# Hybrid Conformer/Mamba-2 layer on one core: stored up products taken into the accumulating bank, down loads and head loads put in another order

## The chip, the cores and the metric

The kernel runs on one core of a Trainium2 chip. The metric is the device time of one execution in microseconds. The engines are TensorE (PE, with PEld for its weight loads), VectorE (DVE), ScalarE (ACT), GpSimd (POOL) and SyncE (SP); SP, ACT and POOL issue DMAs, each from a queue of its own that is worked off in order.

## The reference, cut to what matters

One layer on 1024 positions of 1024 channels, in fp32:

```python
h = layer_norm(x, ln_in_g, ln_in_b)
u = h @ w_in[l]
y_a = conformer_branch(...)          # depthwise conv of 31, norm, product
y_b = ssd_branch(...)                # Mamba-2, 32 heads, chunks of 128
h = layer_norm(DN_ALPHA * h + (sigmoid(gate_a) * y_a + sigmoid(gate_b) * y_b) @ w_o[l], ...)
def conv_ffn(h, w_up, dw_w, dw_b, w_down):        # w_up 1024 x 5632, w_down 2816 x 1024
    u = causal_dwconv(h @ w_up, dw_w, dw_b)       # 3 taps
    gate, val = jnp.split(u, 2, axis=-1)
    return (jax.nn.silu(gate) * val) @ w_down
h = layer_norm(DN_ALPHA * h + conv_ffn(h, ...), ln2_g, ln2_b)
```

## The kernel before, in words

**Arithmetic.** Each fp32 factor is split into a high part (ACT casts it) and a low part (DVE subtracts, L155 and L741), and `mm3` adds three PE products: high x high, high x low, low x high (L166 to L168). A product over 512 input channels, `product`, is thus 12 matmuls of 128x512.

**Stages**, one after the other in the trace: the head (`ln_in(0)`, the norm of x, and `first_columns`), two token mixers with their combinations (to about 1307 us), the sums of h for up (`ffn_blocks`), up, down, and the last norm.

**Up.** The product with `w_up` goes by a 2x2 block scheme with seven products instead of eight. For each of the 22 steps j, `up_rest` works on 128 gate and 128 value columns; `up_weights` loads the rows `ra` and `rb`, forms the weight sums s3, s24 and s10 on DVE and splits them. The products are named by their block of h: b11 and b21 (weights ue), t2 (w_s24), t3 (w_s3), t1 and t4 (w_s10), b22 (w_s24). They share PSUM banks: `acc` banks for b11, t2, t1 and b22 of one step, `sm` banks for t3 and t4. Between two products of one bank a partial result is copied or added out, into `s`, `uv` (value) or `ug` (gate). A step has 84 matmuls. For the first eight steps (LEAD) b11 and b21 are made in `up_first`, while h's other blocks are still being formed, and are stored to DRAM (`first_scr`); those eight steps then take 60 matmuls in `up_rest` and read the two stored halves back. In them t2 has an `sm` bank of its own, and DVE adds the stored half (L871, L877, L885). From step 8 on, one bank carries all and ACT copies (L860, L865, L875, L883). After the products, both halves of u go through a convolution of three taps (L891 on ACT, two L895 on DVE into a buffer `o`, tag "o"), silu (L905) and the gating (L906); of each pair of steps DVE forms sums for down, and POOL's queue stores them as `b11_scr`, `b2_scr`, `t32_scr`, `t41_scr`. The u tiles are a ring of three.

**Down.** Seven products p of eleven steps k each (`down`, `load`). The data of a step come back from the scratch tensors, with a slice of `w_down`, into a raw tile `dr`; `c3` and `c4` keep weight slices for later products. `c3` takes the space of the block of h that b11 and b21 used, `rows` that of t3 and t4, `c4` that of b22, so their first loads wait for the last such matmul. `rows` holds h for the residual, loaded on POOL's queue. The weights are split into `w_dn{p}_{k}`.

**Order.** The program is written in blocks and a scheduler of the framework sets the order of instructions on every engine by its own estimates and by `high_priority` offsets; each engine then works through its list strictly in that order. Tiles come from pools: `tag` and `bufs` say how many buffers rotate, and a new tile waits until the last user of its buffer is done. The pools: `wst` (tag "st", 3 buffers, raw weights), `wsp` (split weights), `up` (o, raw, s, s3), `firsts` (stored products). Space of a closed pool is given to the next, with the same kind of wait.

Of the kernel before, what the change touches and what calls it, by code (L numbers as in the profile page):

```python
# [16 lines left out]
P = 128  # L17
D = 1024
# [38 lines left out]
def kernel(  # L57
# [23 lines left out]
    wsp = ctx.enter_context(tc.tile_pool(name="wsp", bufs=3))  # L81
# [67 lines left out]
    def weights(src, name, pl=None, eng=None, bufs=None):  # L149
        with tc.high_priority(offset=4000):  # L150
            st = wst.tile([P, D], F32, tag="st", name=f"st_{name}")
            SY.dma_start(st, src)
            w = (pl or wsp).tile([P, 2, D], F32R, tag="w", bufs=bufs, name=f"w_{name}")
# [80 lines left out]
    def ln_in(hh):  # L234
        hT = big_tile(f"hT{hh}")
        with pool(f"lnin{hh}", side="right") as pl:
            first = hh == 0
            xts, gb = [], []
            with tc.high_priority(offset=6000):
                for t in range(4):  # L240
# [8 lines left out]
            if first:  # L249
                SY.dma_start(pc[:, :PC_N], pcol)  # L250
# [486 lines left out]
    def split_pair(pl, src, name, n=D, bufs=None, tag="w"):  # L737

        w = pl.tile([P, 2, n], F32R, tag=tag, bufs=bufs, name=f"w_{name}")
# [75 lines left out]
    def up_first(fp, bl, j):  # L815


        w = weights(wup[2 * j], f"ue{j}")
        ps = bank(1)
        for q, block in enumerate(("b11", "b21")):  # L820
            product(ps, lambda i: w[:, i, q * HALF : (q + 1) * HALF], bl[block], q == 0)
            f = fp.tile([P, HALF], F32, tag="first", bufs=4, name=f"first{q}_{j}")
            A.copy(f, ps)
            A.dma_start(first_scr[j][q], f)

    def up_weights(upp, j):


        with tc.high_priority(offset=2000):
            r1 = wst.tile([P, D], F32, tag="st", name=f"ra{j}")  # L830
            SY.dma_start(r1, wup[2 * j])
            if j:
                r2 = upp.tile([P, D], F32, tag="raw", bufs=3, name=f"rb{j}")
# [4 lines left out]
            ue = None if j < LEAD else split_pair(wsp, r1, f"ue{j}")  # L838
# [5 lines left out]
            w24 = split_pair(wsp, r1, f"s24_{j}")  # L844
            w10 = split_pair(wsp, r2, f"s10_{j}")
# [3 lines left out]
    def up_rest(upp, us, bl, j, before):  # L849
# [3 lines left out]
        ue, w24, w10, w3 = up_weights(upp, j)  # L853
# [3 lines left out]
        ps, pz = bank(1 if ue else 0), bank(0)  # L857
        if ue:
# [5 lines left out]
            product(ps, lambda i: w24[:, i, :HALF], bl["t2"], False)  # L864
            A.copy(s, ps)  # L865
        else:
            SY.dma_start(s, first_scr[j][0])
            SY.dma_start(ug[:, early], first_scr[j][1])
            pu = bank(0)
            product(pu, lambda i: w24[:, i, :HALF], bl["t2"], True)  # L870
            V.tensor_tensor(out=s, in0=s, in1=pu, op=ALU.add)  # L871
        product(pz, lambda i: w3[:, i], bl["t3"], True)
        product(ps, lambda i: w10[:, i, :HALF], bl["t1"], not ue)
        if ue:
            A.copy(uv[:, late], ps)  # L875
# [356 lines left out]
```

## Time and profile before

| | |
|---|---|
| median of 3 runs | 2033.85 us (2031.81 to 2035.5) |
| profiled execution | 2035.35 us, span 2033.6 us |
| PE busy | 1978.0 us, 97% of the span |
| DVE busy | 1710.7 us, 84% |
| ACT busy | 1001.8 us, 49% |
| POOL busy | 171.9 us, 8% |
| DMA | 273.51 MB, mean 134 GB/s |
| granted PE clock, mean | 0.991 |

Times in rows count from the start of the span. In a timeline row stand the start, the busy time, the engine, the line of the kernel, the operation, the tile written and the tiles read, the number of instructions, and in brackets the idle time before it with what ended it. A row of a table of windows gives the stretch, its length, each engine's busy time with its instructions, the granted PE clock (1.00 is full speed), the DMA engines' busy share and their rate. A row of waits gives engine and bank, who ended the wait, the total in us, how often, the longest. In rows of the profile the numbers in tile names are left out: `w_s` is any of w_s3, w_s10 and w_s24.

### The profile page before, as it was taken

How to read it: one execution, taken by the hardware profiler on the slowest of the kernel's cores; microseconds unless marked ns; L12 is line 12 of the kernel's file. 1: busy time of each engine (PE TensorE's matmuls, PEld its weight loads, DVE VectorE, ACT ScalarE, POOL GpSimd, SP SyncE). 2: the span in 40 equal slices, each digit the busy share in tenths (PEclk: the TensorE clock that was granted, in tenths of full speed). 3: DMA queues.
4: the chain of work that ended last, by engine and by line, in shares of the span. 5: the costliest groups of instructions: out<-in, count | busy, mean ns of one | idle time of the engine just before them, and what ended most of it. 6: DMA issues, size and time to landing. Idle time of an engine off the chain costs nothing.

```text
span 2033.6 us, 24571 instructions
## 1 busy us (share of the span) xinstructions
PE 1978.0 (97%) x9164; PEld 1628.0 (80%) x9164; DVE 1710.7 (84%) x2285; ACT 1001.8 (49%) x1448; POOL 171.9 (8%) x141
## 2 busy tenths in 40 slices
PE   6999999999999999999999999998899999989998
PEld 6888887888788888888888888887778888777886
DVE  7599999989766869999998976596998788777868
ACT  4465654556453356665454645364334445443432
POOL 2010101001400000100100130010000000010000
PEclk9999999999999999999999999999999999999999
DMA  6212233332546522222423354565342232377563
GB/s 219 93 63 94 79 102 106 99 104 101 174 133 216 195 88 77 88 85 75 127 86 107 109 166 138 188 234 202 130 153 106 99 109 99 109 258 264 175 224 109
DMA packets 97303, 273.51 MB, mean 134 GB/s; under 512 B 11168, under 2 KB 11168, under 8 KB 97184
## 3 DMA queue, kind: packets, MB, share of 16 engines
q1 hardware_dynamic: 87696, 242.06, 35.9%
q0 software_dynamic: 7184, 25.69, 3.3%
q10 hardware_dynamic: 2304, 4.20, 0.6%
q8 instruction: 72, 1.18, 0.2%
q14 instruction: 47, 0.39, 0.1%
HBM read 222.36 MB, written 49.55 MB: 134 GB/s over the span
## 4 chain that ended last, share of the span: by engine, by line
PE 66%; DVE 24%; DMA 4%; issue 4%; ACT 1%; SPq 0%; DVEq 0%; ACTq 0%
PE acc L166 17%; PE acc L168 17%; PE acc L167 17%; DVE c L420 8%; PE sm L166 3%; PE sm L167 3%; PE sm L168 3%; DVE xbc L375 2%; DMA dr<-b_scr 1%; PE acc L357 1%; PE sm L534 1%; DVE fo L895 1%; DMA st_wo<-wo 1%; PE sm L515 1%; DVE w_so L155 1%
## 5 line engine op out<-in xcount | busy, mean ns | idle before, releaser
L420 DVE SCALAR_TENSOR_TENSOR c<-v,pc,c 128x512 f32<-128x512 f32 x480 | 375.3, 805 | 7.6 <-ACT c L409 6.1
L478 POOL TENSOR_TENSOR au<-seg_mv,head_of 128x1024 fp32r<-128x1024 f32 x32 | 76.3, 2383 | 962.2 <-PE sm L487 730.4
L166 PE MATMUL acc<-hT,w_c 128*128 128x512 f32 x352 | 141.1, 401 | 0.0
L167 PE MATMUL acc<-hT,w_c 128*128 128x512 f32 x352 | 140.7, 400 | 0.0
L168 PE MATMUL acc<-hT,w_c 128*128 128x512 f32 x352 | 138.5, 393 | 0.0
L895 DVE SCALAR_TENSOR_TENSOR fo<-u,pc,fo 128x1024 f32<-128x1024 f32 x88 | 111.5, 1279 | 8.5 <-ACT fo L891 7.8
L375 DVE SCALAR_TENSOR_TENSOR xbc<-u,pc,xbc 128x512 f32<-128x512 f32 x144 | 109.7, 774 | 0.7 <-ACT xbc L373 0.5
L167 PE MATMUL acc<-w_z,hT 128*128 128x512 f32 x256 | 100.9, 394 | 0.0
L166 PE MATMUL acc<-w_z,hT 128*128 128x512 f32 x256 | 100.9, 401 | 0.0
L168 PE MATMUL acc<-w_z,hT 128*128 128x512 f32 x256 | 100.7, 396 | 0.0
L1021 ACT CAST w_dn<-dr 128x1024 fp32r<-128x1024 f32 (+1 forms) x73 | 60.8, 842 | 77.7 <-DVE dr L951 31.5
L154 ACT CAST w_c<-st_c 128x1024 fp32r<-128x1024 f32 x50 | 52.5, 1051 | 86.8 <-PE acc L168 66.1
L1022 DVE TENSOR_TENSOR w_dn<-dr,w_dn 128x1024 fp32r<-128x1024 f32 (+1 forms) x73 | 69.6, 963 | 17.6 <-ACT w_dn L1021 17.5
L167 PEld LDWEIGHTS acc<-hT,w_c 128*128 128x128 f32 x352 | 66.2, 188 | 16.8 <-issue 3.8
L168 PEld LDWEIGHTS acc<-hT,w_c 128*128 128x128 f32 x352 | 66.1, 188 | 16.0 <-issue 2.6
L166 PEld LDWEIGHTS acc<-hT,w_c 128*128 128x128 f32 x352 | 66.1, 188 | 15.9 <-issue 2.6
L155 DVE TENSOR_TENSOR w_c<-st_c,w_c 128x1024 fp32r<-128x1024 f32 x47 | 60.6, 1289 | 20.2 <-ACT w_c L154 20.2
L166 PE MATMUL acc<-h1s,w_s 128*128 128x512 f32 x168 | 66.6, 397 | 5.7 <-ACT u L875 5.7
L166 PE MATMUL acc<-h1b,w_ue 128*128 128x512 f32 x176 | 68.9, 392 | 2.6 <-ACT w_ue L740 1.4
L166 PE MATMUL sm<-h1b,w_s 128*128 128x512 f32 x176 | 70.3, 400 | 0.0
L167 PE MATMUL sm<-h1b,w_s 128*128 128x512 f32 x176 | 70.3, 399 | 0.0
L168 PE MATMUL sm<-h1b,w_s 128*128 128x512 f32 x176 | 69.9, 397 | 0.0
(352 smaller groups left out, 5811.1 us busy)
## 6 DMA issues: line engine op xcount, KB each, us to landing
st_c<-wcol SPq DMA_DIRECT2D x50, 512.0 KB, 3.5
st_z<-wz SPq DMA_DIRECT2D x32, 512.0 KB, 3.4
st_wo<-wo SPq DMA_DIRECT2D x24, 512.0 KB, 3.8
ra<-wup SPq DMA_DIRECT2D x22, 512.0 KB, 3.6
rb<-wup SPq DMA_DIRECT2D x22, 512.0 KB, 3.4
t_scr<-fo POOLq DMA_DIRECT2D x22, 512.0 KB, 4.2
dr<-t_scr SPq DMA_DIRECT2D x44, 256.0 KB, 3.4
dr<-wdown SPq DMA_DIRECT2D x38, 256.0 KB, 3.8
```

The source lines that it names most:

```text
L154: A.copy(w[:, 0, :], st)
L155: (eng or V).tensor_tensor(out=w[:, 1, :], in0=st, in1=w[:, 0, :].bitcast(F32), op=ALU.subtract)
L166: TE.matmul(ps, wa(0), xa(0), start=start, stop=False, skip_group_check=more)
L167: TE.matmul(ps, wa(0), xa(1), start=False, stop=False, skip_group_check=more)
L168: TE.matmul(ps, wa(1), xa(0), start=False, stop=stop, skip_group_check=more)
L357: TE.matmul(ps[:, ts], w[:, i, k * P : (k + 1) * P], hT[:, j, k, ts], start=n == 0 and k == 0, stop=n == 2 and k == KD - 1,)
L375: V.scalar_tensor_tensor(out=o, in0=u[:, k : k + HALF], scalar=pc[:, wc + k : wc + k + 1], in1=o, op0=ALU.mult, op1=ALU.add,)
L420: V.scalar_tensor_tensor(out=accs[i], in0=v[:, k : k + HALF], scalar=pc[:, wc + k : wc + k + 1], in1=accs[i], op0=ALU.mult, op1=ALU.add,)
L478: G.tensor_tensor(out=au, in0=seg_mv[:, c, :].unsqueeze(1).to_broadcast([P, 8, P]), in1=head_of[:, g, :].unsqueeze(2).to_broadcast([P, 8, P]),
L895: V.scalar_tensor_tensor(out=o, in0=u[:, k : k + T], scalar=pc[:, wc + k : wc + k + 1], in1=o, op0=ALU.mult, op1=ALU.add,)
L1021: A.copy(w[:, 0, cs], src)
L1022: V.tensor_tensor(out=w[:, 1, cs], in0=src, in1=w[:, 0, cs].bitcast(F32), op=ALU.subtract)
```

## The change

Lines of the changed kernel carry other numbers (mm3 is L173 to L175 there, `split_pair` L754 and L755).

1. **Stored steps.** One DMA brings both stored halves into `ug`; ACT copies the late half into the accumulating bank (L892), t2, t1 and b22 all add into that bank, and ACT copies out between them, as in the later steps. DVE's three additions go.
2. **First weights.** The pool `up` is opened before `up_first`, `up_weights` of step 0 is called before the stored products of step 6, and those of steps 6 and 7 take their weights from `o` buffers. The stored products have 2 buffers instead of 4.
3. **Slots.** The parts in `wsp` get three fixed slots in turn instead of a ring of three; `raw` has 2 buffers instead of 3, `o` 4 instead of 3.
4. **Down.** Raw tiles come from nine buffers (st 3, raw 2, o 4) instead of six; five `c3` slices are copied by GpSimd from `w_st` instead of loaded a second time; the rows come in 16 half tiles at k = 4 of p = 0, 1, 2, 4; the last norm's rows are loaded by POOL's queue at p = 2.
5. **Head.** The norm rows are loaded second and third, ahead of x1; 60 transposes of the identity are put on PE at the start; the first three low weight parts are made by DVE instead of GpSimd.

```diff
+        n_parts[0] += 1
+        return wsp.tile([P, 2, D], F32R, tag=f"w{n_parts[0] % 3}", name=f"w_{name}")
...
-                    if first and t == 1:
+                    if first and t == 0:
                         gb = [row(pl, RW_ING, D, "in_g"), row(pl, RW_INB, D, "in_b")]
...
+                    for i in range(60):
+                        TE.transpose(pt[:, i % 4 * P : (i % 4 + 1) * P], ident, ident)
...
-        ws = [weights(wcol[ct], f"c{hh}_{ct}", eng=None if hh else G) for ct in cts]
+        ws = [weights(wcol[ct], f"c{hh}_{ct}", eng=None) for ct in cts]
...
-            f = fp.tile([P, HALF], F32, tag="first", bufs=4, name=f"first{q}_{j}")
+            f = fp.tile([P, HALF], F32, tag="first", bufs=2, name=f"first{q}_{j}")
...
-        ps, pz = bank(1 if ue else 0), bank(0)
+        ps, pz = bank(1), bank(0)
...
-            product(ps, lambda i: w24[:, i, :HALF], bl["t2"], False)
-            A.copy(s, ps)
         else:
-            SY.dma_start(s, first_scr[j][0])
-            SY.dma_start(ug[:, early], first_scr[j][1])
-            pu = bank(0)
-            product(pu, lambda i: w24[:, i, :HALF], bl["t2"], True)
-            V.tensor_tensor(out=s, in0=s, in1=pu, op=ALU.add)
+            with tc.high_priority(offset=2500):
+                SY.dma_start(
+                    ug[:, 2 : 2 + T].rearrange("p (q n) -> p q n", q=2),
+                    first_scr[j].rearrange("q p n -> p q n"),
+                )
+            A.copy(ps, ug[:, late])
+        product(ps, lambda i: w24[:, i, :HALF], bl["t2"], False)
+        A.copy(s, ps)
         product(pz, lambda i: w3[:, i], bl["t3"], True)
-        product(ps, lambda i: w10[:, i, :HALF], bl["t1"], not ue)
-        if ue:
-            A.copy(uv[:, late], ps)
-        else:
-            V.tensor_tensor(out=uv[:, late], in0=s, in1=ps, op=ALU.add)
+        product(ps, lambda i: w10[:, i, :HALF], bl["t1"], False)
+        A.copy(uv[:, late], ps)
...
         product(ps, lambda i: w24[:, i, HALF:], bl["b22"], False)
-        if ue:
-            A.copy(ug[:, late], ps)
-        else:
-            V.tensor_tensor(out=ug[:, late], in0=s, in1=ps, op=ALU.add)
+        A.copy(ug[:, late], ps)
...
-            o = upp.tile([P, T], F32, tag="o", bufs=3, name=f"fo{jj}")
+            o = upp.tile([P, T], F32, tag="o", bufs=4, name=f"fo{jj}")
...
+            t0, cs = {0: (0, E), 1: (0, L), 2: (4, L), 4: (4, E)}[p]
+            for t in range(t0, t0 + 4):
+                G.dma_start(rs[t][:, cs], h1_scr[t * P : (t + 1) * P, cs])
...
-            pl, tag = ((wst, "st"), (upp, "raw"))[n_raw % 2]
+            pl, tag, n = ((wst, "st", 3), (upp, "raw", 2), (wst, "st", 3), (upp, "o", 4))[n_raw % 4]
...
                 if p == 0 and k < EARLY:
                     SY.dma_start(w_st, a11)
-                    G.dma_start(c3[k], a11)
+                    G.tensor_copy(c3[k], w_st)
...
-                if k == 2 and p in (0, 2):
-                    load_rows(range(2 * p, 2 * p + 4))
+                if k == 4 and p in (0, 1, 2, 4):
+                    load_rows(p)
...
     with pool("firsts", side="right") as fp:
         for j in range(LEAD):
-            up_first(fp, bl, j)
+            if j == LEAD - 2:
+                ws = up_weights(upp, 0)
+            up_first(upp, fp, bl, j)
```

What this does to the order on three engines. First PE in the fourth stored step (j = 3), at t1 (weights w_s10_3, block h1s2). Before, it starts a bank of its own behind step 2's t4:

```order
L167 MATMUL sm516_11432<-h1b2_10852,w_s10_2_11424 128x512
L168 MATMUL sm516_11432<-h1b2_10852,w_s10_2_11424 128x512
L166 MATMUL sm518_11531<-h1s2_10449,w_s10_3_11524 128x512 [waits DVE_49,Activation_49]
L167 MATMUL sm518_11531<-h1s2_10449,w_s10_3_11524 128x512
L168 MATMUL sm518_11531<-h1s2_10449,w_s10_3_11524 128x512 [waits DVE_49]
```

Now it stands right behind t2 in the same bank (acc516):

```order
L174 MATMUL acc516_11591<-h1s3_10511,w_s24_3_11581 128x512
L175 MATMUL acc516_11591<-h1s3_10511,w_s24_3_11581 128x512
L173 MATMUL acc516_11591<-h1s2_10510,w_s10_3_11584 128x512 [waits Activation_49]
L174 MATMUL acc516_11591<-h1s2_10510,w_s10_3_11584 128x512
L175 MATMUL acc516_11591<-h1s2_10510,w_s10_3_11584 128x512 [waits DVE_49]
```

ACT's copy of s now lies between two neighbours on PE. Second, SP's queue at the start of down (dr_k is the raw tile of the k-th down step, counted from 1; each is filled by a load of data and, for the first five, one of weights). Before:

```order
L979 DMA dr_4_13948<-b11_scr3_137 128x512
L981 DMA dr_4_13948<-wdown 128x512
L979 DMA dr_3_13925<-b11_scr2_136 128x512
L981 DMA dr_3_13925<-wdown 128x512
L985 DMA c3_13866<-wdown 128x512 x6
L979 DMA dr_6_13986<-b11_scr5_139 128x512
L979 DMA dr_5_13967<-b11_scr4_138 128x512
L981 DMA dr_5_13967<-wdown 128x512
L979 DMA dr_7_14006<-b11_scr6_140 128x512
L988 DMA c4_0_13868<-wdown 128x512
```

Now, from c4_0 on (ahead of it stand dr_2, dr_4, five c3 loads, dr_1, dr_5, dr_6 and dr_9):

```order
L1013 DMA c4_0_13919<-wdown 128x512
L1013 DMA c4_1_13920<-wdown 128x512
L1013 DMA c4_2_13921<-wdown 128x512
L1013 DMA c4_3_13922<-wdown 128x512
L1013 DMA c4_4_13923<-wdown 128x512
L1013 DMA c4_5_13924<-wdown 128x512
L1004 DMA dr_8_14077<-b11_scr7_141 128x512
L1013 DMA c4_6_13925<-wdown 128x512
L1004 DMA dr_10_14117<-b11_scr9_143 128x512
L1013 DMA c4_7_13926<-wdown 128x512
L1004 DMA dr_3_13976<-b11_scr2_136 128x512
L1006 DMA dr_3_13976<-wdown 128x512
```

dr_3, whose tile is an `o` buffer now, has moved from ahead of the c3 loads to behind eight of the c4 loads. Third, ACT at the same place, with the cast of w_dn0_2 from dr_3. Before:

```order
L1021 CAST w_dn0_7_14029<-c3_13866 128x512 [waits DMAHW0_49]
L883 COPY u0_11200<-acc572_13739 128x512
L1021 CAST w_dn0_2_13929<-dr_3_13925 128x1024 [waits DMAHW5_49,PE_49]
L891 ACTIVATE fo21_13833<-u0_11200,pc_107 128x1024 [waits DMASW4_49,Activation_49]
L891 ACTIVATE fo43_13837<-u1_11201,pc_107 128x1024 [waits DVE_49]
L1021 CAST w_dn0_4_13971<-dr_5_13967 128x1024 [waits DMAHW6_49,DMAHW5_49,PE_49]
```

Now:

```order
L902 COPY u0_10969<-acc565_13794 128x512
L908 ACTIVATE fo21_13888<-u0_10969,pc_107 128x1024 [waits DMASW6_49,Activation_49]
L908 ACTIVATE fo43_13892<-u1_10970,pc_107 128x1024 [waits DMASW7_49,DVE_49]
L1045 CAST w_dn0_4_14018<-dr_5_14014 128x1024 [waits DMAHW3_49,DMAHW2_49,PE_49]
L1045 CAST w_dn0_6_14060<-c3_13917 128x512 [waits PE_49]
L1045 CAST w_dn0_7_14080<-dr_8_14077 128x512 [waits DMAHW4_49]
L922 ACTIVATE fo21_13888<-fo21_13888,pc_107 128x1024 [waits DVE_49]
L1045 CAST w_dn0_2_13980<-dr_3_13976 128x1024 [waits DMAHW1_49,DMAHW0_49]
```

The cast has moved behind the last step's convolution outputs and silu. On PE, w_dn0_2's matmuls follow those of w_dn0_0 and w_dn0_1 in both kernels.

More of the change, by code (lines that the diff above doesn't have):

```diff
@@ L249, in ln_in @@
             if first:
+                with tc.high_priority(offset=8000):
+                    pt = bank(1)
+                    for i in range(60):
+                        TE.transpose(pt[:, i % 4 * P : (i % 4 + 1) * P], ident, ident)
                 SY.dma_start(pc[:, :PC_N], pcol)
@@ L832, in up_weights @@
             if j:
-                r2 = upp.tile([P, D], F32, tag="raw", bufs=3, name=f"rb{j}")
+                r2 = upp.tile([P, D], F32, tag="raw", bufs=2, name=f"rb{j}")
             else:
@@ L1013, in load @@
                     own = n_steps % 2 and n_steps > 2
[L1014 to L1016 removed]
+                    nm = f"w_dn{p}_{k}"
+                    w = dp.tile([P, 2, D], F32R, tag="w", bufs=3, name=nm) if own else part_tile(nm[2:])
                 cuts = ((slice(0, D), st),) if w_st is not c3[k] and w_st is not c4[k] else (
@@ L1118 @@
         bl = ffn_blocks(tp, qp, mixT)
-    with pool("firsts", side="right") as fp:
-        for j in range(LEAD):
-            up_first(fp, bl, j)
     upp = ctx.enter_context(pool("up"))
@@ L1125 @@
         G.memset(u[:, :2], 0.0)
+    with pool("firsts", side="right") as fp:
+        for j in range(LEAD):
+            if j == LEAD - 2:
+                ws = up_weights(upp, 0)
+            up_first(upp, fp, bl, j)
     before = None
     for j in range(NF):
-        before = up_rest(upp, us, bl, j, before)
+        before, ws = up_rest(upp, us, bl, j, before, ws), None
     ffn_stack.close()
     dp = ctx.enter_context(pool("down", side="right"))
-    g, b = row(dp, RW_2G, D, "ln2_g"), row(dp, RW_2B, D, "ln2_b")
-    down(upp, dp, g, b)
+    down(upp, dp)
 _OUT = "out_0_dram"
```

61 lines of the change are left out of this document (38 added, 23 removed).

## Prediction

> **What bounds the kernel now.** I read the page first (PE is busy for 97% of the span, so only stretches in which PE loses matmuls are worth anything), then a table of windows of 25 us, then PE's waits, and last the timelines around the places found. All rows are of the profiled execution of the kernel before, 2035.35 us with a span of 2033.6; the median of the runs is 2033.85, 1.5 us lower, and a difference found here is applied to that median. A run can tell a change from none at 0.2%, about 4.1 us.
>
> ```profile
> core 0: us, PE busy (x) PEld busy (x) DVE busy (x) ACT busy (x) POOL busy (x), PEclk, DMA share, GB/s
> 1375.00:1400.00 25.00, 23.84 (x110) 19.48 (x109) 15.34 (x21) 13.09 (x23) 2.73 (x5) 1.00 0.63 225
> 1400.00:1425.00 25.00, 19.70 (x75) 15.61 (x74) 17.51 (x25) 6.09 (x8) 0.00 (x0) 0.86 0.46 158
> 1425.00:1450.00 25.00, 23.16 (x99) 18.09 (x98) 22.49 (x26) 12.89 (x12) 0.73 (x1) 1.00 0.34 113
> 1450.00:1475.00 25.00, 21.12 (x84) 16.86 (x83) 23.34 (x30) 6.69 (x7) 2.15 (x4) 0.90 0.42 155
> 1475.00:1500.00 25.00, 24.27 (x103) 19.53 (x102) 23.50 (x29) 10.08 (x10) 1.59 (x3) 0.97 0.49 165
> 1500.00:1525.00 25.00, 23.36 (x103) 18.90 (x102) 24.39 (x30) 10.08 (x11) 1.44 (x3) 1.00 0.42 138
> ...
> 1775.00:1800.00 25.00, 23.88 (x106) 19.40 (x104) 17.61 (x21) 10.49 (x13) 4.31 (x8) 1.00 0.59 200
> 1800.00:1825.00 25.00, 20.68 (x83) 16.69 (x84) 21.89 (x24) 14.59 (x20) 4.80 (x9) 0.86 0.72 261
> 1825.00:1850.00 25.00, 22.50 (x91) 17.83 (x90) 16.28 (x26) 9.44 (x17) 1.60 (x3) 0.93 0.88 329
> 1850.00:1875.00 25.00, 25.00 (x112) 20.69 (x111) 22.26 (x34) 9.74 (x14) 0.00 (x0) 1.00 0.78 240
> ```
>
> A full window holds 112 matmuls of 128x512 (the last row), so one costs 25/112 = 0.223 us. From 1375 to 1525, the start of up and the steps fed from stored products, PE issues 574 of 672: 98 are missing, 21.9 us. From 1775 to 1850, where up ends and down begins, 280 of 336: 56 missing, 12.5 us. These two stretches are all that the up and down parts of the change can win; the waits name what opens the holes.
>
> ```profile
> PE sm L166 <- DVE u L877: 7.0, 3, 3.9
> PE sm L166 <- ACT w_s L740: 6.0, 2, 5.3
> PE acc L166 <- ACT u L875: 5.7, 2, 5.4
> ```
>
> **Part 1, the start of up and the eight stored steps.** The first hole is the cast of the first `w_s3`; its tiles lie in space that the last stored products still held.
>
> ```profile
> 1405.84 0.79 PE L166 MATMUL sm<-h1s,w_s 128*128 128x512 f32 x1 [5.30 <-ACT w_s L740]
> 1402.21 0.69 DVE L741 TENSOR_TENSOR w_s<-s,w_s 128x512 fp32r<-128x512 f32 x1 [9.94 <-ACT w_s L740]
> L877 DVE TENSOR_TENSOR u<-s,sm 128x512 f32<-128x512 f32 x7 | 4.8, 684 | 0.6 <-PE sm L168 0.6
> ra<-wup SPq DMA_DIRECT2D x22, 512.0 KB, 3.6
> ```
>
> DVE stood idle for 9.94 us here. With the pool opened earlier that time serves the first weights, and the hole of 5.3 us with its slow matmuls goes. What is late next is the low part of `ue1_6`: it now follows s3 and the sum in `rb0` on DVE, and st_ue7's load waits for a slot of `st`; I allow 2 us (bounds 0 and the old 5.3).
>
> In each of the eight steps DVE loses L871, L877 and L885: 24 x 0.684 = 16.4 us of an engine that is 22.5 to 24.4 us busy in a window of 25. These are off the path except where PE waits for L877. ACT gains four copies of about 0.59 us a step (row of L875 below, 128x512), 19 us over eight steps on an engine that is at most 13.1 us busy in those windows. But each copy now stands between two products of one bank, and PE's order puts t1 the next product right behind the one that is copied out at three places of the stored steps (j = 1, 3, 5) and two matmuls behind it at four (j = 3 to 6). The trace has that case once, at the end of step 19.
>
> ```profile
> 1769.10 0.39 PE L167 MATMUL acc<-h1s,w_s 128*128 128x512 f32 x1
> 1769.76 0.50 PE L166 MATMUL acc<-h1s,w_s 128*128 128x512 f32 x1 [0.28 <-ACT u L875]
> 1769.12 0.59 ACT L875 COPY u<-acc 128x512 f32<-128x512 f32 x1 [1.68 <-PE acc L168]
> ```
>
> Starts 0.66 us apart instead of 0.223: 0.44 us for two matmuls between, so 0.44 + 2 x 0.223 = 0.88 with none. Three times 0.88 and, in the stored steps, four times 0.44 make 4.4 us.
>
> The remaining term is a chain that comes round every two steps. I add it up with the durations of such rows as the ones shown here and below: on DVE 1.2 for 1024 columns (two passes in 2.48) and 0.6 for 512 in a row of them, on ACT 1.15, 1.05 and 0.6. From the low part of an even step's w_s10: this and two passes (3.6), on ACT the silu, the next convolution output, the cast of w_s3 and the copy of s (3.5), on PE t1, ten matmuls of s3 and b22 (34 x 0.223 = 7.6), and on ACT the cast of the next w_s10 into the slot that b22 has left (1.1): 15.8. From there, in the odd step: six operations of 1024 and two of 512 columns on DVE up to the second pass over uv of step j-2 (8.4), the load of both halves, which SP can issue only then (512 KB, as ra: 3.6), the copy into PSUM (0.6) and the cast behind it on ACT (1.05): 13.6. Together 29.4, or 14.7 a step, against 13.4 for 60 matmuls and 0.6 of the gaps above: 0.7 x 6 = 4.2 us more (bounds: 0, if the loads come early; 10, if DVE stays the bound as now). Sum: 2 + 4.4 + 4.2 = 10.6, say 11 of the 21.9 us stay; **-11** (-16 to -5). Three slots for the parts and two for raw only shift loads: covered by this slack of about 2 us.
>
> For j of 8 and more the code is as before, but four more places have two matmuls between (10, 13, 16, 20, with 19 as before): 4 x 0.44, **+2** (0 to +3).
>
> **Part 2, from up to down.** The second hole is an ACT that stands at a convolution output because its `o` buffer waits for stores of step 19.
>
> ```profile
> 1798.77 1.15 ACT L891 ACTIVATE fo<-u,pc 128x1024 f32<-128x1024 f32 x1 [4.06 <-DMA b_scr<-fo]
> 1801.51 1.15 ACT L891 ACTIVATE fo<-u,pc 128x1024 f32<-128x1024 f32 x1 [1.59 <-DMA t_scr<-fo]
> 1804.27 0.79 PE L166 MATMUL acc<-h1s,w_s 128*128 128x512 f32 x1 [5.39 <-ACT u L875]
> 1804.86 0.63 PE L167 MATMUL acc<-h1s,w_s 128*128 128x512 f32 x1
> ...
> 1807.42 0.53 PE L167 MATMUL acc<-h1s,w_s 128*128 128x512 f32 x1
> ```
>
> After such a hole eight matmuls come 0.43 us apart (six from 1804.86 to 1807.42), 1.7 us more. With four `o` buffers this wait goes: step 20's first output needs no store, only its second waits for a store of step 19, and between c3's space coming free, which those stores follow on POOL, and ACT's wait PE has 64 matmuls, 14 us; I count the store as landed by then. But look at what SP does. `dr_3`, the data of the third down step, is given an `o` buffer, and its load now stands behind the c4 loads, which wait for the space of the last b22 product (call its end T; 1808.9 here). Before, it was loaded 34 us ahead of T, and its cast ran without a wait at 1812.86.
>
> ```profile
> SPq L988 <- PE acc L168: 14.0, 1, 14.0
> 1775.16 0.33 SPq L979 DMA_DIRECT2D dr<-b_scr  x1
> 1808.91 2.70 SPq L988 DMA_DIRECT2D c<-wdown  x6
> 1812.86 1.05 ACT L1021 CAST w_dn<-dr 128x1024 fp32r<-128x1024 f32 x1
> 1819.93 0.63 ACT L1021 CAST w_dn<-dr 128x512 fp32r<-128x512 f32 x1 [1.96 <-DMA dr<-b_scr]
> 1823.85 0.62 ACT L1021 CAST w_dn<-dr 128x512 fp32r<-128x512 f32 x1 [2.25 <-DMA dr<-b_scr]
> 1831.65 0.62 ACT L1021 CAST w_dn<-dr 128x512 fp32r<-128x512 f32 x1 [4.76 <-DMA dr<-b_scr]
> ```
>
> PE reaches `w_dn0_2` 27 matmuls after T (12 of t4, 15 of the first two down steps): T + 6.0. The last three rows are the 7th, 9th and 13th transfer of SP after T, of 256 KB each: 11.0, 14.9 and 22.7 us after T, 1.95 us apiece. `dr_3`'s two halves become the 11th and 12th: T + 20.8 at that pace, since the rows move at the same time on POOL's queue (1809 to 1832):
>
> ```profile
> q1 hardware_dynamic: 2033, 4.01, 51.3%
> q0 software_dynamic: 1124, 4.08, 44.6%
> rows<-h_scr POOLq DMA_DIRECT2D x8, 512.0 KB, 12.4
> ```
>
> The rows become half tiles, so they will crowd SP less, and 2.25 MB (five c3 copies, two norm rows) no longer go by DMA near here. Alone, the 3.1 MB through `dr_3` at the rate of these 23 us (8.1 MB, 352 GB/s) would land near T + 10. I take T + 17, nearer to the measured pace. Cast 1.05 and handover 0.1: PE waits 12.1 us, and 1.7 us of slow matmuls follow. To this come 1.8 (at j = 21 t2, t1 and b22 follow each other without a matmul between: 2 x 0.88) and 0.7 (`dr_1` now behind five c3 loads): 16.3 against 12.5, **+4** (-3 with T + 10, +8 with T + 20.8). The c3 copies on GpSimd cost at most what its sums of that shape take:
>
> ```profile
> L627 POOL TENSOR_TENSOR mean<-mean,cc 128x512 f32<-128x512 f32 x12 | 19.0, 1587 | 2.9 <-DMA cc<-c_scr 2.1
> ```
>
> Three stand ahead of step 19's stores on POOL, 4.8 us, under some 23 us of up that PE still has then; if they took 3 us longer, ACT would wait for the store again. The norm rows of the last layer norm are used 150 us later.
>
> The Trainium skill, "DMA: Bandwidth & Descriptors", section on queues, rings and completion order, says that an engine takes turns between queues packet by packet. The trace agrees: 4.01 MB in 2033 packets on SP's queue against 4.08 MB in 1124 on POOL's, with SP getting the smaller share while both were full. By it halved rows raise SP's share from 0.35 (packets of 1.97 KB against 3.63) to 0.5, 1.37 us apiece, and with two landed before the rows start `dr_3` would be there at T + 16.7, and the sum 0.3 us lower.
>
> **Part 3, the head.**
>
> ```profile
> 8.83 2.48 DVE L227 SCALAR_TENSOR_TENSOR x<-x,mv_in,in_g 128x1024 f32<-128x1024 f32 x2 [1.58 <-DMA in_g<-prow]
> 17.99 5.12 DVE L227 SCALAR_TENSOR_TENSOR x<-x,mv_in,in_g 128x1024 f32<-128x1024 f32 x2
> 16.31 9.06 POOL L155 TENSOR_TENSOR w_c<-st_c,w_c 128x1024 fp32r<-128x1024 f32 x3 [13.87 <-ACT w_c L154]
> ```
>
> The norm rows a place earlier save at most the wait of 1.58. Three low parts move to DVE, 3 x 1.2 = 3.6 us, and POOL no longer doubles DVE's passes beside it (5.12 against 2.48, and some of L230): even. Sixty transposes end before x0's are due at about 10 us or delay them by a few us, while DVE's passes over x2 and x3 set the end. **-0.5** (-2 to +1).
>
> **Sum**: -11 + 2 + 4 - 0.5 = -5.5: 2029.85 for the profiled execution, 2028.4 for the median.
>
> **Rivals.**
> - A, much faster. `dr_3` is there when PE comes, since c4's space comes free by an earlier product than b22's in the new layout of the pools, so that T lies some 10 us earlier for SP: the 13.8 us of Part 2 go, 2014.6. Against it speaks that L988 waited for b22 and that c4 keeps its place in the program; for it, that the two norm rows that lay ahead of c4 in that space are gone.
> - B, no change. The pace of 1.95 us holds (T + 20.8, +3.8): 2032.2. The same comes out if the chain of Part 1 eats its gain (+4 to +5). For it: both queues were full for 20 us.
> - C, slower. ACT's queue becomes the bound of the stored steps: the copy into PSUM waits for a load, and everything behind it on ACT (w_s10's cast, u's copies, the convolution) stands too. Each us over 14.7 a step costs 7; from 1.4 us over it the whole is slower by more than 4.1, at 2 us it is 2042. For it: ACT already waited for DVE and DMA in the rows above; against it: DVE gets 16.4 us of room.
>
> **How the numbers follow.** Forecast 0.40 (faster by 4 to 11), A 0.14, B 0.24, C 0.16, and 0.06 for a slower outcome by something unseen (loads in down with other slots). Faster 0.54, same 0.24, slower 0.22. The forecast's own range is 2023 to 2030; the range for 8 in 10 takes in A's 2014.6 and most of C: 2014 to 2040.
>
> **What would show it.** In the profile after: no wait of PE for w_s at the first s3 and no slow matmuls after it, some 620 matmuls between 1375 and 1525; small waits of PE for ACT s and u, 0.4 to 0.9 us each; no ACT wait of 4 us for b_scr before the end of up; and a hole in PE of 8 to 15 us at the third down step, released by ACT's cast of `w_dn`, itself waiting for dr<-b_scr. If that hole is missing, A holds; if PE's waits for ACT in the stored steps add to over 12 us, C. Wrong altogether would be a new hole in a place where nothing was lost before, in the mixers or after 1850.

## The result: 12 us slower

The changed kernel takes 2046.6 us (median of 4, 2044.9 to 2050.6), the kernel before 2034.7 beside it: a ratio of 1.0062, 95% interval 1.0042 to 1.0082. The forecast was 2028.4, and its range ended at 2040. The profiled execution after takes 2044.85 us with a span of 2043.2.

The windows of 25 us after, with the columns as before:

```profile
core 0: us, PE busy (x) PEld busy (x) DVE busy (x) ACT busy (x) POOL busy (x), PEclk, DMA share, GB/s
1375.00:1400.00 25.00, 22.09 (x91) 16.36 (x90) 20.44 (x29) 15.68 (x25) 1.80 (x5) 1.00 0.80 262
...
1425.00:1450.00 25.00, 21.61 (x86) 17.23 (x87) 22.70 (x27) 13.26 (x16) 1.23 (x2) 0.93 0.40 133
...
1800.00:1825.00 25.00, 10.94 (x47) 8.36 (x45) 14.41 (x16) 9.95 (x13) 9.27 (x17) 0.83 0.76 265
1825.00:1850.00 25.00, 21.90 (x88) 17.71 (x89) 13.39 (x20) 8.99 (x16) 2.23 (x4) 0.90 0.74 263
1850.00:1875.00 25.00, 25.00 (x112) 20.67 (x112) 19.95 (x33) 10.58 (x17) 0.55 (x1) 1.00 0.60 198
```

The window behind the end of up holds 47 matmuls of 112 (83 before); the one from 1425 holds 86 (99 before). PE's waits after, the largest of up and down:

```profile
PE acc L173 <- ACT w_dn L1045: 17.5, 2, 15.2
PE sm L173 <- ACT w_s L754: 4.4, 5, 1.6
PE acc L173 <- ACT u L897: 4.0, 2, 3.3
PE acc L173 <- ACT s L894: 3.5, 7, 0.8
PE acc L173 <- ACT w_s L754: 3.4, 4, 1.0
```

VectorE's `u`, which led the list before, is gone; ScalarE leads it, and the cast of one down weight alone costs 15.2 us. The rows of SP, ACT and PE around it:

```profile
1805.58 2.71 SPq L1013 DMA_DIRECT2D c<-wdown  x6
...
1812.18 0.33 SPq L1004 DMA_DIRECT2D dr<-b_scr  x1
1812.86 0.33 SPq L1006 DMA_DIRECT2D dr<-wdown  x1
...
1825.77 1.04 ACT L1045 CAST w_dn<-dr 128x1024 fp32r<-128x1024 f32 x1 [8.36 <-DMA dr<-wdown]
...
1811.28 0.39 PE L175 MATMUL acc<-w_dn 128*128 128x512 f32 x1
1826.87 1.65 PE L173 MATMUL acc<-w_dn 128*128 128x512 f32 x3 [15.20 <-ACT w_dn L1045]
```

The c4 loads start at 1805.58 (T); `dr_3` is issued behind eight of them and its cast starts at T + 20.2.

To compare kernels whose stages shift, I count PE's matmuls from the first product of `w_ue` on (2788 to the end in every kernel) and add up by how much starts lie further apart than 0.2236 us (distances over 0.28). Up to matmul 240 is the start of up, to 660 the stored steps, to 1740 steps 8 to 20, to 1872 the end of up (its last product), to 2300 the first part of down; behind 2300 nothing is lost anywhere. Ratios are to the kernel before in the same comparison, whose medians lie between 2032.9 and 2034.7.

| kernel | median us | ratio (95%) | 0-240 | 240-660 | 660-1740 | 1740-1872 | 1872-2300 |
|---|---|---|---|---|---|---|---|
| before | 2034.7 | | 10.2 | 12.6 | 2.3 | 7.3 | 5.0 |
| after | 2046.6 | 1.0062 (1.0042-1.0082) | 5.6 | 13.9 | 8.0 | 4.6 | 18.6 |
| e1, no o for down | 2045.2 | 1.0069 (1.0056-1.0083) | 5.4 | 13.8 | 7.9 | 4.5 | 18.0 |
| e2, ring | 2043.9 | 1.0058 (1.0046-1.0071) | 3.6 | 15.2 | 10.1 | 0.5 | 19.3 |
| e3, both | 2045.9 | 1.0066 (1.0054-1.0079) | 4.3 | 16.1 | 10.1 | 0.5 | 20.1 |
| e4, head only | 2031.6 | 0.9990 (0.9981-0.9999) | 10.0 | 12.4 | 2.2 | 7.1 | 5.4 |
| e5, before, two raw | 2036.5 | 1.0018 (1.0008-1.0029) | 0.5 | 13.8 | 1.7 | 6.9 | 17.0 |
| e6, three raw, ring | 2051.9 | 1.0087 (1.0070-1.0105) | 24.3 | 16.0 | 10.4 | 0.5 | 2.3 |
| e7, stored steps only | 2038.4 | 1.0020 (1.0010-1.0030) | 4.9 | 12.6 | 10.4 | 5.8 | 4.9 |
| e8, after without them | 2032.9 | 1.0003 (0.9993-1.0014) | 5.7 | 7.4 | 2.5 | 4.0 | 17.7 |
| e9, e8 and half slots | 2017.0 | 0.9919 (0.9906-0.9932) | 5.8 | 7.9 | 2.7 | 3.3 | 1.3 |
| e10, four stored steps | 2032.3 | 0.9993 (0.9982-1.0003) | 4.9 | 15.4 | 2.2 | 8.9 | 3.6 |
| e11, before, half slots | 2027.6 | 0.9969 (0.9958-0.9979) | 0.6 | 15.4 | 1.7 | 7.0 | 8.2 |
| e12, e11 with four o | 2020.1 | 0.9937 (0.9925-0.9949) | 10.7 | 8.3 | 5.3 | 0.5 | 3.2 |
| e13, e9, copy into bank | 2021.8 | 0.9939 (0.9925-0.9953) | 6.6 | 11.9 | 4.0 | 3.2 | 1.7 |
| e14, after, half slots | 2027.3 | 0.9966 (0.9953-0.9978) | 5.3 | 13.8 | 9.5 | 2.3 | 1.5 |

After against before: -4.6, +1.3, +5.7, -2.7 and +13.6, together +13.3. Ahead of the first `w_ue` product profiles scatter (it starts between 1348.6 and 1353.3 us, in kernels with the head edit and without), so the stages are compared and not the spans. A profiled run need not be the median one either: that of e7 took 2034.46 us, that of e12 2023.04.

### The profile page after: what moved, and what is told of

It is laid out like the page before. It is cut to its first block, busy times and chain, and to the rows that moved or that the text cites. A ratio compares the mean times of both kernels' runs of the same rounds, so it can differ in the third digit from the quotient of the medians.

```text
span 2043.2 us, 24653 instructions
## 1 busy us (share of the span) xinstructions
PE 1985.5 (97%) x9224; PEld 1629.8 (80%) x9224; DVE 1698.6 (83%) x2264; ACT 1019.8 (50%) x1480; POOL 171.9 (8%) x148
## 4 chain that ended last, share of the span: by engine, by line
PE 66%; DVE 23%; issue 4%; DMA 3%; ACT 3%; SPq 0%; POOL 0%; ACTq 0%; DVEq 0%; POOLq 0%
PE acc L173 17%; PE acc L175 17%; PE acc L174 17%; DVE c L431 8%; PE sm L173 3%; PE sm L175 3%; PE sm L174 3%; PE acc L368 2%; DVE xbc L386 2%; PE sm L545 1%; DVE fo L912 1%; DMA dr<-wdown 1%; DMA st_wo<-wo 1%; PE sm L199 1%; PE sm L526 1%
## 5 line engine op out<-in xcount | busy, mean ns | idle before, releaser
L173 PE MATMUL acc<-hT,w_c 128*128 128x512 f32 x352 | 141.0, 401 | 0.0
L175 PE MATMUL acc<-hT,w_c 128*128 128x512 f32 x352 | 138.4, 393 | 0.0
L173 PE MATMUL acc<-h1s,w_s 128*128 128x512 f32 x264 | 105.5, 400 | 11.6 <-ACT u L897 4.0
L175 PE MATMUL acc<-h1s,w_s 128*128 128x512 f32 x264 | 104.1, 394 | 1.6 <-DVE w_s L755 1.6
L174 PE MATMUL acc<-h1s,w_s 128*128 128x512 f32 x264 | 103.6, 392 | 0.0
L173 PE MATMUL acc<-w_z,hT 128*128 128x512 f32 x256 | 100.8, 401 | 0.0
L175 PE MATMUL acc<-w_z,hT 128*128 128x512 f32 x256 | 100.7, 396 | 0.0
L162 DVE TENSOR_TENSOR w_c<-st_c,w_c 128x1024 fp32r<-128x1024 f32 x50 | 64.0, 1282 | 20.2 <-ACT w_c L161 20.2
L173 PE MATMUL acc<-w_dn 128*128 128x512 f32 x160 | 62.2, 397 | 17.5 <-ACT w_dn L1045 17.5
L175 PEld LDWEIGHTS acc<-hT,w_c 128*128 128x128 f32 x352 | 66.1, 188 | 16.1 <-issue 2.6
L173 PEld LDWEIGHTS acc<-hT,w_c 128*128 128x128 f32 x352 | 66.1, 188 | 16.0 <-issue 2.6
L173 PE MATMUL sm<-h1b,w_s 128*128 128x512 f32 x176 | 69.7, 396 | 4.4 <-ACT w_s L754 4.4
```

Of the source, the lines that this page charges most:

```text
L162: (eng or V).tensor_tensor(out=w[:, 1, :], in0=st, in1=w[:, 0, :].bitcast(F32), op=ALU.subtract)
L173: TE.matmul(ps, wa(0), xa(0), start=start, stop=False, skip_group_check=more)
L174: TE.matmul(ps, wa(0), xa(1), start=False, stop=False, skip_group_check=more)
L175: TE.matmul(ps, wa(1), xa(0), start=False, stop=stop, skip_group_check=more)
```

## Experiments

**First theory: two accidents, the o slot of `dr_3` and the fixed slots of the parts (e1, e2, e3), and the head by itself (e4).** A line of a diff can stand for several places; `...` marks what is left out of it.

```diff
- ((wst, "st", 3), (upp, "raw", 2), (wst, "st", 3), (upp, "o", 4))[n_raw % 4]
+ ((wst, "st", 3), (upp, "raw", 2))[n_raw % 2]                        # e1, e3
- wsp.tile([P, 2, D], F32R, tag=f"w{n_parts[0] % 3}", ...)
+ wsp.tile([P, 2, D], F32R, tag="w", bufs=3, ...)                     # e2, e3
```

> The changed kernel, but the loads of the down steps take turns between st and raw alone; none goes into an o buffer, so dr_3 is again issued ahead of the c4 loads. Theory (the 15.59 us hole of PE at the third down step, with the half clock behind it, comes from dr_3 standing behind c4 in SP's queue): the hole goes, of PE's 17.5 us of waits for the casts of w_dn at most 4 stay, and the time is 13 to 17 us below the changed kernel: 2030 to 2034. Rival (the loads around the end of up are late because SP's and POOL's queues are both full, wherever dr_3 stands): a hole of 8 us or more stays at one of the first four down steps, and the time is above 2038.

> The changed kernel, but the weight parts take the next free slot of a ring of three again, in place of three fixed slots in turn. Theory (steps 8 to 21 lost 7.4 us against before because a fixed slot ties the cast of a weight part to the one part that held this slot, and sets products of one bank two matmuls apart): the waits of PE for ACT's s, u and w_s in steps 8 to 21 fall to what they were before, 5 to 8 us are won, 2038.5 to 2041.5; the hole at the third down step stays at 14 to 17 us. Rival (the loss of these steps comes from the four o buffers and two raw buffers): no change, 2045 to 2048.

> Both edits: the ring for the weight parts, and no o buffer for the down loads. If the two losses are separate places and add, 19 to 23 us below the changed kernel: 2024 to 2028, which is 7 to 11 us below the kernel before. If one only moves the other (weights that come earlier meet the same late loads), 2030 to 2034.

> The kernel before with the head's part of the change alone: norm rows loaded second, sixty transposes of the identity at the start, low parts of the first weights on VectorE. Theory (the head is worth what the start of the first 128x512 product showed, -0.28 us): 2033.5 to 2034.5, no change that can be measured. Rival (the 2.6 us that the changed kernel was ahead at 660 us come with this part as well, through another order of VectorE's passes there): 2030.5 to 2032.

Both theories fell. In e1 `dr_3` is ahead of c4 and its hole is gone, but the loss in down stays (18.0 against 18.6):

```profile
PE acc L173 <- ACT w_dn L1045: 10.3, 4, 7.1
PE acc L174 <- DVE w_dn L1046: 3.0, 2, 2.1
...
1827.68 0.62 ACT L1045 CAST w_dn<-dr 128x512 fp32r<-128x512 f32 x1 [7.83 <-DMA dr<-b_scr]
```

The hole moved from the third to the seventh down step (`dr_7`), and a second one opened some 87 us after T. So the loads are one too few, whichever of them stands behind c4. The ring of e2 makes steps 8 to 20 no better (10.1), and e3, with both edits, lies outside both of its ranges. The head is worth 1.4 us, within what a run can tell; the median of e4 lies in the range of its rival, and PE's wait for VectorE's `x` at 662 us (1.13 us in the kernel before) is indeed gone in e4.

**What raw has to do with it (e5, e6).** e5 is the kernel before with one thing taken away; e6 is the changed kernel with three raw, for which the copies of the first products move into the slots of `s`, with the ring of e2 and the down loads in st and raw in turn.

```diff
- tag="raw", bufs=3          # up_weights of before; raw() of the down loads likewise
+ tag="raw", bufs=2          # e5
- f = fp.tile([P, HALF], F32, tag="first", bufs=2, ...)
+ f = upp.tile([P, HALF], F32, tag="s", bufs=2, ...)    # e6, with raw bufs=3
```

> The kernel before with two raw buffers instead of three, in up and for the down loads, and nothing else. Theory (the changed kernel loses because one raw buffer went: one down load fewer is ahead of the c4 loads, six b11_scr rows where there were seven, and a 2D step of two loads waits for the slot again later): PE loses 4 to 8 us more within 40 us of the end of up, as the variant without o for the down loads did, and 3 to 8 us some 85 us after it; together 7 to 14 us slower than before, 2040 to 2047. Rival (the lost buffer is covered; what costs is the order of the casts or the row loads): within 2 us of before.

> The changed kernel with three raw buffers beside the four o buffers: the copies of the first products take the slots of s, so that the pool firsts goes and its space holds the third raw. The weight parts stand in a ring of three, and the down loads take st and raw in turn. Theory (the third raw buffer is what the changed kernel lacks): the holes at the third down step, 14 us after the end of up and 85 us after it go (PE's waits for the casts of w_dn under 5 us), while ScalarE's wait for b_scr stays away: against the kernel before 3 to 4 us won in the stored steps, 6 to 7 at the end of up, 0 to 8 lost in steps 8 to 21: 2023 to 2032. Rival (the losses at the down steps come from elsewhere): 2038 or more.

In down both came out as the theory said: two raw cost the kernel before 12.0 us there (17.0 against 5.0), three raw bring the changed kernel to 2.3 (e3, with the ring and the down loads as in e6 but two raw, loses 20.1). Of e5, the casts that PE waits for:

```profile
PE acc L166 <- ACT w_dn L1021: 5.5, 4, 1.8
PE sm L166 <- ACT w_dn L1021: 4.8, 1, 4.8
```

The totals came out otherwise. e5 is only 3.5 us slower than before, because the hole at the first `w_s3` closed by itself (0.5 against 10.2): without the third raw the pool of up is 4 KB smaller, and these tiles, as I read it, no longer lie on the space of the last stored products. No run prints where tiles lie, but e11 and e12 below bear it out: their one difference is a fourth o buffer of the same 4 KB, and the hole is closed in the first (0.6) and open in the second (10.7). e6 loses 24 us at the start of up; in its order the first copies of stored products stand on ScalarE behind the last casts of the blocks (one such wait of PE is 10.8 us). That was my edit's fault, and says nothing on the change.

**The stored steps by themselves (e7) and the change without them (e8).** In e7 `up_rest` alone is the changed one; in e8 all is changed but it: two loads, t2 and t1 in banks of their own, VectorE's three sums.

> The kernel before with the stored steps of the changed one: one load of both halves, the stored product copied into the accumulating bank by ScalarE, no passes of VectorE over s. Prediction on record: these copies free VectorE of 16.4 us, and the waits for its u go. If so, 5 to 10 us less than before in the stored steps: 2023 to 2028. Rival from the cumulative losses (between the 240th and the 660th matmul of up the changed kernel loses 13.8 us, before 12.7): the edit wins nothing by itself, since waits for ScalarE's s and u and for the casts behind them take the place of those for VectorE: 2031 to 2035.

> The changed kernel, but with the stored steps of the kernel before (two loads, products into a bank of their own, sums by VectorE); the early first weights, the slots and the down part stay as changed. If the stored-step edit wins nothing, the losses up to the 660th matmul of up stay at 17 to 22 us and the time at 2043 to 2049, unless the other order of the loads moves the hole at the third down step. If it is what won 11 us, 2055 or more.

e8 is the run that turned the study. Without the stored-step edit the stored steps lose 7.4 us in place of 13.9, and steps 8 to 20, which the edit does not touch, 2.5 in place of 8.0; the whole is 13.7 us faster than the changed kernel by the medians, 12 by the ratios; both ranges of the expectation had it slower. In e7 the loss in the first hole falls from 10.2 to 4.9, that in steps 8 to 20 rises from 2.3 to 10.4, and that in the stored steps stays at 12.6; its median lies above both of its ranges.

The lead of e8 over before in the stored steps (7.4 against 12.6) goes with another part of the change, as the table shows: with the old stored steps, kernels of three o buffers lose 12.4 to 15.4 us there (before, e4, e5, e11), those of four 7.4 to 8.3 (e8, e9, e12), and e12 differs from e11 by the fourth o alone and has the first weights as before. How that buffer does it was not tried.

**What carries the loss into steps 8 to 20 (e10).** The order of PE's instructions is fixed before the run. In steps 8 and on the code is the same in all kernels but for the buffers, but the order is a pattern that repeats, and the stored steps set which one. The pattern around the start of `ue.14` (matmuls in brackets; t4.12 is step 12's fourth product):

```
before, e10: b22.12(11) t4.12(12) b22.12(1) t2.13(12) ue.14(24)
e7, e2:      t2.13(10) b22.12(11) t4.12(12) b22.12(1) t2.13(2) ue.14(4)
```

In e7 `ue` follows three matmuls behind t4. ScalarE casts w_s10 only when t4 has ended, and the cast of `w_ue` stands behind that one; ACT and PE of e7, and its waits from 1525 to 1785 us:

```profile
1599.23 1.05 ACT L740 CAST w_s<-rb 128x1024 fp32r<-128x1024 f32 x1 [9.71 <-PE sm L168]
1600.18 1.04 ACT L740 CAST w_ue<-ra 128x1024 fp32r<-128x1024 f32 x1
...
1601.28 0.50 PE L166 MATMUL acc<-h1b,w_ue 128*128 128x512 f32 x1 [1.40 <-ACT w_ue L740]
...
PE acc L166 <- ACT w_ue L740: 8.4, 6, 1.4
```

e10 edits steps 0 to 3 only; its order from step 8 on is that of the kernel before.

```diff
-        else:                       # e7: all eight stored steps
+        elif j < 4:                 # e10: steps 4 to 7 as before
```

> The kernel before with the stored-step edit in steps 0 to 3 alone; steps 4 to 7 are as before. Theory (the 8 us that steps 8 to 21 lose in each kernel with this edit come from the order of the products in which the last stored steps leave the loop: here the order of steps 12 to 14 is word for word that of the kernel before): the losses between the 660th and the 1800th matmul of up fall from 10.9 us (all eight steps edited) to 1.5 to 4, and the time is 2028 to 2033. Rival (something that the edit leaves in the later steps, such as banks or buffers): they stay at 8 or more, 2036 or more.

The losses of steps 8 to 20 fall from 10.4 to 2.2, and of six waits one is left, as before:

```profile
PE acc L166 <- ACT w_ue L740: 1.4, 1, 1.4
```

So the order carries them. The changed kernel follows a third order, in which it is casts of w_s that stand close ahead of their products; its waits in the same stretch:

```profile
PE acc L173 <- ACT w_s L754: 2.5, 3, 1.0
PE acc L173 <- ACT s L894: 1.4, 4, 0.8
```

Why the planner falls into the one pattern or the other was not tried; a fourth o buffer alone is enough to tip it (e12 below).

**Seven loads ahead of c4 with two raw (e9, e11, e12, e14).** The down loads from the sixth on need 512 columns, a slot of `s`.

```diff
+ if n_raw in (6, 8):
+     t = upp.tile([P, HALF], F32, tag="s", bufs=2, ...)
+ st, rw, o = (wst, "st", 3), (upp, "raw", 2), (upp, "o", 4)
+ (st, rw, st, rw, st, None, st, None, rw)[n_raw - 1] if n_raw < 10 else (st, rw, st, o)[n_raw % 4]
```

> The variant of the changed kernel with the stored steps of before, and one thing more: the down loads that need 512 columns only (the sixth and the eighth) go into the slots of s, and no o slot is used by the first nine. With that seven down loads stand ahead of the c4 loads again, with two raw buffers as before. Theory (the hole at the third down step is the order of SP's queue, one load too few ahead of c4): PE's loss from the end of up on falls from 17.8 us to 3 to 6, so 12 to 15 us under the variant without these slots (2032.9): 2018 to 2021. Rival (the two queues are full after the end of up whatever the order, and another load is late instead): a hole of 7 us or more stays within 25 us of it, 2025 to 2030.

> The kernel before with two raw buffers, the same slots for the down loads (the sixth and eighth in s, then st, raw and o in turn), and the head of the changed kernel; the first weights, the stored steps and the three o buffers as before. From the losses of the variant with two raw buffers (14 us to the 660th matmul, where before loses 23, 2 in steps 8 to 21, 7 at the end of up, 17 after it) with the last one down to 3 to 6: 11 to 14 us under that variant's 2036.5, and 1 to 3 for the head: 2020 to 2025. If the losses after the end of up do not come from the number of loads ahead: 2031 or more.

> The same with a fourth o buffer. At the end of up ScalarE no longer waits for b_scr: 5 us won there. But from step 14 on the order of the products is the one in which the ring variants lost 1.6 us every second step, so 5 to 6 us are lost there: within 3 us of the variant with three o buffers. If the order does not matter, 4 to 6 us under it.

> The changed kernel with the slots of the best variant for the down loads, and nothing else (the stored-step edit stays). If the two losses add (13.6 us from the stored-step edit as found, 16 us from the down loads): 2046.6 - 16 = 2030.6, in 2028 to 2033, so no better than the kernel before. PE's waits for the casts of w_dn under 3 us, and the losses up to the 1800th matmul as in the changed kernel, 29 to 32 us. If the stored-step edit costs only together with the late down loads: 2017 to 2022.

The first row is e8's longest wait for a cast of `w_dn`, the second e9's; then SP of e9 ahead of its c4 loads:

```profile
PE acc L173 <- ACT w_dn L1050: 14.0, 1, 14.0
```

```profile
PE acc L173 <- ACT w_dn L1054: 0.5, 1, 0.5
...
1783.65 3.75 SPq L1013 DMA_DIRECT2D dr<-b_scr  x3
1787.44 0.42 SPq L1015 DMA_DIRECT2D dr<-wdown  x1
1794.92 2.71 SPq L1022 DMA_DIRECT2D c<-wdown  x6
```

With seven steps' data ahead, down loses 1.3 us (e9) and 1.5 (e14), and e9 is the fastest kernel of the study, 0.81% under before. The four kernels with and without each remedy nearly add: of the changed kernel's 50.6 us lost, the stored-step edit's share is 13.2 (to 37.4 in e8), that of the late loads 18.2 (to 32.4 in e14), both 29.6 (to 21.0 in e9). e14 is a little better than expected. e11 misses by 3 us: two down loads of its are still late (8.2). e12 misses too: against e11 the order cost 3.6 us in steps 8 to 20, where 5 to 6 were expected, the fourth o won 6.5 at the end of up, where I had counted 5, and down lost 5.0 less. Two changes had no term at all: the first hole opened again (10.1 more) and the stored steps lost 7.1 less.

**Which part of the stored-step edit costs in the stored steps (e13).** One third of it put back into e9: the one load and the copy into the bank of t2; t1 and b22 as before.

```diff
+            A.copy(ps, ug[:, late])
+            product(ps, lambda i: w24[:, i, :HALF], bl["t2"], False)
+            A.copy(s, ps)
+            ps = bank(0)        # t1, b22; VectorE adds s
```

> The best variant so far (2017.0: stored steps of before, seven down loads ahead) with one third of the stored-step edit put back: one load of both halves, the stored product copied into the bank of t2 by ScalarE, t2 added to it there. The products t1 and b22 stay in a bank of their own and VectorE adds s to them, so no product stands behind a copy out of its own bank after t1. Theory (what the stored-step edit costs in the stored steps is ScalarE's copies of u and s between products of one bank, each of which stands in ScalarE's queue behind convolution outputs): the losses up to the 660th matmul of up stay at 11 to 14.5 us, and PE's waits for ScalarE there under 4 us; the order of later steps has two more near neighbours, 1 to 3 us: 2015 to 2020. Rival (the cost is the late load and the copy into the bank): 17 us or more up to there, 2021 or more.

The losses to 660 are 18.5: the rival's number. But PE waits for VectorE's `u` now, as in the kernel before; of e13, the stretch from 1395 to 1520 us, and ACT and DVE ahead of the longest wait:

```profile
PE sm L173 <- DVE u L903: 7.2, 5, 3.5
...
1457.73 1.14 ACT L917 ACTIVATE fo<-u,pc 128x1024 f32<-128x1024 f32 x1
1458.78 0.56 ACT L896 COPY s<-acc 128x512 f32<-128x512 f32 x1
...
1459.07 1.28 DVE L921 SCALAR_TENSOR_TENSOR fo<-u,pc,fo 128x1024 f32<-128x1024 f32 x1
1460.26 0.68 DVE L865 TENSOR_TENSOR ra<-ra 128x512 f32<-128x512 f32 x1
1460.87 0.68 DVE L903 TENSOR_TENSOR u<-s,sm 128x512 f32<-128x512 f32 x1
```

The copy of s waits on ScalarE behind a convolution output, and VectorE takes its sum after two more passes. So the copy into and out of t2's bank is already as dear as the whole edit; that ScalarE's copies behind t1 and b22 are the cost, as I held, is not borne out. How much is the chain and how much the other order of VectorE stays open.

## Why the prediction was wrong, step by step

Two steps failed: the gain that Part 1 credits to the stored-step edit, and the price of nothing for the third raw in down. Besides, the order from step 8 on cost more than its term.

**Part 1 (-11; measured -3.3).** The counts of instructions were right: VectorE has 24 fewer and ScalarE 32 more, four copies a step. The first row is of e8, which has the old stored steps, the second of the changed kernel:

```profile
PE 1981.8 (98%) x9224; PEld 1629.7 (80%) x9224; DVE 1709.0 (84%) x2288; ACT 1003.7 (49%) x1448; POOL 170.1 (8%) x148
PE 1985.5 (97%) x9224; PEld 1629.8 (80%) x9224; DVE 1698.6 (83%) x2264; ACT 1019.8 (50%) x1480; POOL 171.9 (8%) x148
```

VectorE is busy 10.4 us less (12.1 in e14 against e9), where the prediction had 16.4: two passes in a row start 0.61 us apart though each takes 0.68 (1460.26 and 1460.87 in e13 above), which is part of the difference. The step that failed is to credit the edit with the waits for VectorE. With four o buffers most of them go without it (7.4 us lost in the stored steps of e8), a gain that the sum did not have, and the edit then costs 6.5 there (e8 to the changed kernel) and 5.9 (e9 to e14); with three o it wins nothing in these steps (12.6 in e7 and before). So its costs, priced at 4.4 for copies and 4.2 for the chain, came, and its gain did not. From 1375 to 1525 the changed kernel has 583 matmuls; the prediction asked for some 620.

Of the 13.9 us of the stored steps 7.1 are lost at one place, 4.9 at four waits for casts of `w_s`, and 1.9 at two copies of s, 0.95 each where 0.88 was priced. The start of up kept 5.6 us, not 2. The place of the 7.1 us (matmuls 300 to 360) is the first time round the chain, for which the sum had no term; ACT and PE of the changed kernel:

```profile
1424.32 2.19 ACT L908 ACTIVATE fo<-u,pc 128x1024 f32<-128x1024 f32 x2
1426.53 1.28 ACT L922 ACT_TABLE_LOAD   x1
1429.28 1.15 ACT L922 ACTIVATE fo<-fo,pc 128x1024 f32<-128x1024 f32 x1 [1.47 <-DVE fo L912]
1430.33 0.57 ACT L897 COPY u<-acc 128x512 f32<-128x512 f32 x1
...
1427.29 0.39 PE L175 MATMUL acc<-h1s,w_s 128*128 128x512 f32 x1
1430.95 0.80 PE L173 MATMUL acc<-h1s,w_s 128*128 128x512 f32 x1 [3.28 <-ACT u L897]
1431.55 0.63 PE L174 MATMUL acc<-h1s,w_s 128*128 128x512 f32 x1
```

I priced a copy between neighbours at 0.88, as if ScalarE were free. Here it stands behind two convolution outputs, the load of silu's table, a wait for VectorE and the silu: 3.67 between starts, and slow matmuls behind it (0.43 us apart). The same ACT rows in e8 and e9 cost nothing, since no product waits for a copy there. The Trainium skill, "ScalarE: Activation LUTs", section "What ACT_TABLE_LOAD costs", gives about 1283 ns for the load; the row's 1.28 agrees. The steady chain itself was nearly right: two steps take 30.8 us (ScalarE's first convolution outputs start at 1453.75 and 1484.59), predicted 29.4. Rival C came near and missed its own mark: PE's waits for ScalarE from 1395 to 1520 are 10.1 us, and it asked for over 12.

**Steps from 8 on (+2; measured +5.7).** "The code is as before" was true, and the products two matmuls apart cost about what I said (four waits for s, 1.4 us, with the matmuls behind them 2.6). What I left out is that another repeating order also sets casts and the products that need them side by side (e7 against e10): three waits for `w_s` make 5.0 of the changed kernel's 8.0.

**Part 2 (+4; measured +10.9, of it -2.7 at the end of up and +13.6 in down).** ScalarE's wait for b_scr went, and the hole stood where it was forecast. The landing was mis-sized: T + 20.2, where I took 17 between bounds of 10 and 20.8, so the old pace of rival B was nearly right; the wait was 15.2 and not 12.1, and `dr_1`, behind the c3 loads, cost 2.6 and not 0.7. But the step that failed is this sentence: "Three slots for the parts and two for raw only shift loads: covered by this slack of about 2 us." I looked for that cover in up. In down the third raw was the slot of the seventh load ahead of c4, and it is worth 12 us (e5). The 0.06 for "loads in down with other slots" named the place, without a price. Had `dr_3` not been late, another load would have been (e1). The half rows did not help as the sum by the Trainium skill, "DMA: Bandwidth & Descriptors", section "Queues, rings and completion order", would have it (T + 16.7): the packets on POOL's queue did not halve. From 1805 to 1828 us after:

```profile
q1 hardware_dynamic: 2079, 3.80, 49.8%
q0 software_dynamic: 1107, 3.66, 42.5%
```

That is 3.31 KB a packet, 3.63 before. The turns themselves held: from 1817 to 1828 us POOL's queue got 811 packets and SP's 807 before, 841 and 840 after. SP's share of the bytes was 1.48 of 4.46 MB before and 1.52 of 4.29 MB after; what failed was to take the packets as halved with the rows.

**Part 3 (-0.5).** e4 says -1.4 with an interval from -3.9 to -0.2: right within what can be told.

## What to carry to other kernels

Count buffers at each place that borrows them: a slot which the code's own stage can spare may be the one that a later stage prefetches with, and its price shows there. A wait that one edit is credited with may go by another edit of the same change: here the fourth o buffer took most of the waits for VectorE, and the stored-step edit was left with its costs. So price each edit with the others in place. And when an order is planned ahead, a small edit changes stages that it does not touch: compare the repeating part of the order before trusting "the code is as before".

## What was not expected of the hardware

Both DMA queues are busy for some 23 us after T (324 GB/s after, 338 in e9), and e9, which moves as much at the same place, loses only 1.3 us in down, since what PE needs first is already there. In these kernels the order of issue counted, not the traffic. And splitting 512 KB row loads in two halves of their columns left the packets of the queue at over 3 KB (above), so the other queue's share hardly moved, though the two took turns packet by packet almost exactly.
